# Differential attention in a two-layer trunk: score products that all use 128 rows, and heads that start one by one

## The chip, the cores and the metric

One core of a Trainium2 chip runs the whole kernel in one launch. The metric is the device time in microseconds of one execution. "Before" is the median of three runs.

## What is computed

Two layers, each a mixer of three parallel branches (a convolution module, a short gated convolution, differential attention with rotary positions) and an MLP, both with RMS norms and modulation by a conditioning vector. There are 512 tokens of width 1024, all in float32. The change touches the attention:

```python
N_HEADS = 8; HEAD_DIM = 64; V_HEAD_DIM = 128; Q_BLOCK = 128; DEPTH = 2

def diff_attention(q, k, v, lam, subln_g, lambda_init):
    # q, k: (1, 512, 8 heads, 2 parts, 64), turned by apply_rope before; v: (1, 512, 8, 128)
    for i in range(seq // Q_BLOCK):
        lo, hi = i * Q_BLOCK, (i + 1) * Q_BLOCK
        qb, kb, vb = q[:, lo:hi], k[:, :hi], v[:, :hi]
        s = jnp.einsum('bqhcd,bkhcd->bhcqk', qb, kb) * scale
        p = jax.nn.softmax(jnp.where(mask, s, -jnp.inf), axis=-1)
        a = p[:, :, 0] - lam * p[:, :, 1]
        outs.append(jnp.einsum('bhqk,bkhd->bqhd', a, vb))
    o = rmsnorm(jnp.concatenate(outs, axis=1), subln_g) * (1.0 - lambda_init)
```

Each head thus has two parts of 64 features, with a score matrix for each part, and block i of 128 queries sees the first 128 (i + 1) keys.

## The kernel before

**Products.** Activations lie with features on the partitions and the 512 tokens along the free axis. A float32 operand is split into a high part (rounded to float32r) and a low part (the rest), and a product is made of three passes: high x high, high x low, low x high. A projection of 128 output features takes 8 k-tiles x 3 passes = 24 matmuls of 512 columns into one of three PSUM banks, tag `mm`. Nearly all of them are issued in the helper `mm`, line 145, so they carry that line whatever they belong to. Weights come as raw tiles of 256 columns by DMA from SP's queue (line 367) and are split into `wh` (ScalarE, line 394) and `wl` (VectorE, line 402), with three tiles of each.

**Order.** The order of all five engines is the order of emission in Python. `mm` counts columns; each 4096 of them make a step (`STEP`), which is 8 matmuls of 512 columns. Everything that goes beside the projections is a generator in a heap of tasks: `yield n` means "not before n steps from now". So a task's place in every engine's queue follows from steps, and no engine reorders what was emitted.

**Queries and keys.** A layer's mixer goes through four pairs of heads. For each pair it makes four projections (queries and keys of the first head, then of the second) and the values. Each projection is followed by the task `rope`: ScalarE copies the PSUM bank out (line 712), four small DMAs swap halves (714), VectorE turns (717 to 720), ScalarE casts the high parts (723 and 724). To use all 128 rows of TensorE, for each part c the tile `d`c of the queries holds the high part twice, one copy above the other, and that of the keys holds the high part above the low part (or below it). One matmul of 128 rows is then high x high + high x low. The copies into the other half of the partitions are DMAs of 64 x 512 on SP (734 and 735). The low part of the queries lies once, both parts in one tile `lo` (728).

**Scores.** `attend` is the task of one head. For each of the four query blocks, and for each part c, it issues line 786 (128 rows, as above) and line 787: the queries' low part against the keys' high part, both 64 rows, on the half of the partitions where part c lies. Both sum into one bank of tag `s`, of which there are two, one for each part. After each block it stays away for `QSTEP` = 2 steps. `softmax` then reads the banks with VectorE (line 750, which frees them) and goes on with ScalarE (757) and VectorE (762 to 766). Then come the transposed weights (803), the products with the values (814, twelve of them, three for each key tile: 512, 384, 256 and 128 columns) and the norm of the head (822, 455).

**When a head begins.** The local task `pair` waits until all four tiles of the pair are there, then (first pair) `FIRST` = 2 more steps; it starts the first head, and `PERIOD` = 9 steps later the second. In layer 1 three projections (`NF`) are already made in the closing part of layer 0.

**Slots.** Tiles of tag `qk` take 16 slots in turn: a head uses five (two `d` and `lo` for queries, two `d` for keys), and a new tile waits until the one that had its slot 16 tiles ago has been read.

Of the kernel before, what the change touches and what calls it, by code (L numbers as in the profile page):

```python
# [10 lines left out]
F32 = mybir.dt.float32  # L11
# [12 lines left out]
NH = 8  # L24
# [6 lines left out]
# order of emission: columns of a step; steps between an event and what follows it  # L31
# [3 lines left out]
# the start: k-tiles of scale and shift of each quarter whose products VectorE makes, and the order  # L35
# [13 lines left out]
# the end of a sub-layer and the start of the next: the order  # L49
# [14 lines left out]
# columns of the per-layer parameter tile  # L64
C_BADA, C_NMIX, C_NMLP, C_CAB, C_LNG, C_LNB, C_CBW, C_SUB, C_FG = 0, 48, 56, 64, 68, 72, 76, 88, 89
NROW = 97
# order of the six adaLN vectors
# [4 lines left out]
def kernel(  # L72
# [46 lines left out]
    # ---------------------------------------------------------------- order of emission  # L119
    # Instructions are emitted in the order in which the engines run them. The products drive  # L120
    # a count of steps of STEP columns; what goes beside them waits in tasks, generators that
    # yield how many steps to stay away.
# [20 lines left out]
    def mm(ps, lhsT, rhs, start, stop, n):  # L143
        """a matrix product of the main stream"""
        T.matmul(ps, lhsT, rhs, start=start, stop=stop)  # L145
        clock[2] += n
        if clock[2] >= STEP:
            clock[2] -= STEP
            step()

    def pacer(p):
        """steps to wait, on average p() of them"""
        left = 0.0
        while True:
            left += p()
            n = int(left)
            left -= n
            yield n

    # ---------------------------------------------------------------- constants  # L160
# [17 lines left out]
    # ---------------------------------------------------------------- parameters  # L178
# [3 lines left out]
    def params(l, eng=None):  # L182
        """parameters by feature: rows in, transposed"""
# [42 lines left out]
    # lambda of the differential attention: -lambda on all partitions  # L226
# [29 lines left out]
    # ---------------------------------------------------------------- adaLN  # L256
# [5 lines left out]
    def ada_done(l, q, n, sm):  # L262
        """bias and what follows, of n of the columns of ada from column q"""
        v = q // 8
        dst = ada[l][:, q : q + n]
        ada_known[l].update(range(q, q + n))
        assert (l, 1 if v == SC_F else 0) in written and (l, 0) in written
        V.tensor_tensor(dst, sm, prm[l][:, C_BADA + q : C_BADA + q + n], op=ALU.add)
        if v in (SC_M, SC_F):
            f = (0 if v == SC_M else 8) + q % 8  # L270
            g0 = (C_NMIX if v == SC_M else C_NMLP) + q % 8
            V.scalar_tensor_tensor(out=gsc[l][:, f : f + n], in0=dst, scalar=1.0,
                                   in1=prm[l][:, g0 : g0 + n], op0=ALU.add, op1=ALU.mult)
        if v == G_M:
            V.tensor_scalar(out=dst, in0=dst, scalar1=0.5, scalar2=None, op0=ALU.mult)
# [8 lines left out]
    def ada_task(vs, pace):  # L284
        """task: vectors (layer, which) of adaLN, the products on VectorE, the sums over the
        partitions after a transpose"""
# [42 lines left out]
    # ---------------------------------------------------------------- weights  # L329
# [23 lines left out]
    # the raw tiles of 256 columns, and the halves of them in the order of their use  # L353
# [17 lines left out]
    def w_split(extra=None):  # L371
        """the next half of a raw tile as two parts; extra: a tag of
        slots that holds one beside the three of the pool"""
# [5 lines left out]
        if kk < 0:  # L379
            # the halves are rows  # L380
# [36 lines left out]
    def proj(ps, w, act, t0=0, t1=S, k0=0, k1=None):  # L417
        """a product, three passes of every k-tile"""
# [15 lines left out]
    # ---------------------------------------------------------------- helpers of the norms  # L434
    def rsqrt_small(v, n):
        """1/sqrt(v) for a small tile of positive numbers"""
        y = stile(n)
        G.tensor_tensor(y, v[:, :n], nhalf[:, :n], op=ALU.pow)  # L438
        return y

    def colsum(tiles, w, t0=0, t1=S):
        """means over the partitions of the tiles, tokens on partitions"""
# [8 lines left out]
    def bcast(col, n):  # L451
        """columns [tokens, n] to rows along all partitions, in PSUM"""
# [10 lines left out]
    def split(src, res, tags=("qk", "qk")):  # L463
        """task: src as two parts, put into the list res"""
# [7 lines left out]
    # ---------------------------------------------------------------- norm of x and modulation  # L472
    xT = [xpool.tile([P, S], F32, name=f"xT{k}") for k in range(KD)]

    def modulate(l, f, rb, hh, ks, t0=0, t1=S):
        """h tiles (hi, lo) of tokens t0:t1 from the broadcast 1/rms"""
# [25 lines left out]
    def sumsq(e, acc, t0, t1):  # L502
        """task: adds the squares of x tile e to acc"""
# [8 lines left out]
    def closing(lg, v, act, l, f, evac):  # L512
        """The product that closes a sub-layer, its residual gated by vector v of layer lg, and
        the norm of sub-layer f of layer l after it. The last two output tiles go in halves of the tokens, as do the first
        NF tiles of what follows, so that the norm of one half runs beside the products of the
        other. Returns h; evac takes the first tiles' products."""
# [84 lines left out]
    # ---------------------------------------------------------------- the end  # L601
    o2 = out.rearrange("b s d -> (b s) d")

    def ending_prepare(g):
        """task: x by token, and the rows of the last gains along all partitions"""
# [25 lines left out]
    def ending(act):  # L631
        """the last product, with the tokens on partitions, its residual, the last norm"""
# [70 lines left out]
    # ---------------------------------------------------------------- attention  # L703
# [3 lines left out]
    def rope(pp, res, j):  # L707
        """task: a tile of queries (j even) or keys (odd), turned. Queries: per part the high
        part twice one above the other, and the low part of both; keys: per part high and low
        part one above the other."""  # L710
# [15 lines left out]
        if j % 2 == 0:  # L726
            lo = slot("qk", F32R)
            V.tensor_tensor(lo, u, d0.bitcast(F32), op=ALU.subtract)
            src = (d0, d1)
        else:  # L730
            lo = u.bitcast(F32R)
            V.tensor_tensor(lo, u, d0.bitcast(F32), op=ALU.subtract)
            src = (u, u)
        nc.sync.dma_start(d0[64:, :].bitcast(F32), src[0][:64, :].bitcast(F32))
        nc.sync.dma_start(d1[:64, :].bitcast(F32), src[1][64:, :].bitcast(F32))
        yield RWAIT
        res.append((d0, d1, lo))
# [4 lines left out]
    def softmax(l, i, sps, l0, a):  # L742
        """task: query block i of a head"""
# [21 lines left out]
        # (softmax 0 - lambda softmax 1) times the sum of softmax 0  # L765
# [10 lines left out]
    def attend(l, hd, q, k, v, res):  # L776
        """task: one head"""
        a = []
        l0 = stile(4)
        for i in range(NTB):  # L780
# [3 lines left out]
            for cc in range(2):  # L784
                r = slice(64 * cc, 64 * cc + 64)
                T.matmul(sps[cc][:, :n], q[cc][:, blk], k[cc][:, :n], start=True, stop=False)  # L786
                T.matmul(sps[cc][:, :n], q[2][r, blk], k[cc][r, :n], start=False, stop=True)  # L787
# [3 lines left out]
        # transposed weights, keys on partitions  # L791
# [37 lines left out]
        # the mean square and eps, both times the squared sum of softmax 0  # L829
# [13 lines left out]
    # ---------------------------------------------------------------- mixer  # L843
    def mixer(l, h, qk, nfirst):
        """qk: the list for the first pair's queries and keys, nfirst of them under way"""
        oh = [None] * NH
        oo, glu, cv, yb, ya = [], [], [None] * 4, [], []
        # --- queries, keys, values
        for hp in range(NH // 2):
            if hp:  # L850
                qk, nfirst = [], 0
            for j in range(nfirst, 4):
                product(h, rope, qk, j)
            wv = [getw(), getw()]
            v2 = []
# [13 lines left out]
            def pair(hp, qk, v2):  # L869
                while len(qk) < 4:  # L870
                    yield 1
                if hp == 0 and FIRST:
                    yield FIRST
                spawn(attend(l, 2 * hp, qk[0], qk[1], v2, oh))
                yield PERIOD
                spawn(attend(l, 2 * hp + 1, qk[2], qk[3], v2, oh))

            spawn(pair(hp, qk, v2))
            run_due()

# [9 lines left out]
        # --- conformer convolution: gated linear unit  # L890
# [22 lines left out]
        def conv_norm():  # L913
            """layer norm of the convolution and its silu"""
# [66 lines left out]
        # --- short gated convolution  # L981
# [33 lines left out]
        # --- gates and merge  # L1015
# [34 lines left out]
    # ---------------------------------------------------------------- MLP  # L1050
# [9 lines left out]
    def mlp(l, h, f, nfirst):  # L1060
        """f: the list for the first hidden tiles, nfirst of them under way; returns the last"""
# [21 lines left out]
    # ---------------------------------------------------------------- the trunk  # L1083
# [6 lines left out]
    # --- the start: x by feature, and the first norm as fast as its adaLN vectors come in  # L1090
# [16 lines left out]
    def fetch(v, qt):  # L1107
        """a quarter of an adaLN vector: k-tiles 2j, 2j + 1 of 256 columns in tile j"""
# [23 lines left out]
    # rotary tables  # L1132
# [7 lines left out]
    def angles():  # L1140
        """task: the angles within half a turn; the cosine is the sine of a quarter turn more"""
# [26 lines left out]
    def partial(qt, vs):  # L1168
        """the products of the last k-tiles of a quarter, on VectorE; v: scale, shift"""
# [13 lines left out]
    def rows_of(qt, v, pt):  # L1183
        """sums over the partitions along all partitions, with the products of the other k-tiles"""
# [8 lines left out]
    def turn(row):  # L1193
        """by feature"""
# [26 lines left out]
    def warm(n):  # L1221
        """keeps TensorE's clock up while it has nothing to do"""
# [15 lines left out]
    # the first four chunks of weights: two parts, a quarter of their k-tiles at a time  # L1238
# [133 lines left out]
```

## Time and profile before

| | |
|---|---|
| Runs | 1935.61, 1937.01, 1938.61 us (median 1937.01) |
| Profiled execution: span from first to last instruction | 1935.4 us; the page gives no time of its own beside it |
| TensorE busy (PE) | 1914.2 us, 99% |
| VectorE (DVE), ScalarE (ACT), GpSimd (POOL) | 1246.5, 787.5, 60.6 us |
| Attention stage of layer 0 and of layer 1 | about 65 to 315 us and 1002 to 1262 us after the start |
| DMA moved | 236.99 MB, mean 122 GB/s |

PE is TensorE's matmuls, PEld its weight loads, which may run beside a matmul, SPq the DMA issues of SP. In rows by form, `64*128 64x512` is a weight tile of 64 rows and 128 columns with 512 columns that move through it, and the last columns are busy us, mean ns of one, and idle us ahead with what ended it. In the chain the columns are the start, the us that the piece adds to the path, and what it is. A wait for several semaphores is put down to the one that came last by the profile, which can be the wrong one when the engine named had long been done.

### The profile page before, as it was taken

The page shows a single profiled execution, that of the slowest core. Times are in us where ns is not written, and L with a number is a line of the kernel's source. Part 1 is how long each engine was busy: PE and PEld are TensorE (multiplying, and loading weights), DVE is VectorE, ACT ScalarE, POOL GpSimd, SP SyncE. Part 2 cuts the span into 40 slices and gives each one's busy share as a digit, 9 for nine tenths or more (in the row PEclk, how much of TensorE's full clock was granted, in tenths as well). Part 3 has the DMA queues.
Part 4 walks back from the last instruction along what each step waited for, and adds up shares of the span by engine and source line. Part 5 has one row for each costly group of instructions (what it writes and reads, how often), then busy time and mean ns, then how long its engine had stood idle before and what let it go on. Part 6 is the DMA issues. An engine that isn't in the chain of part 4 may idle for free.

```text
span 1935.4 us, 24880 instructions
## 1 busy us (share of the span) xinstructions
PE 1914.2 (99%) x9565; PEld 1602.8 (83%) x9565; DVE 1246.5 (64%) x2123; ACT 787.5 (41%) x1420; POOL 60.6 (3%) x109
## 2 busy tenths in 40 slices
PE   8999999999999999999999999999999999999998
PEld 6788878888889888888898788888888898888888
DVE  7776688997766656565676776898654563333335
ACT  4555553222433524243444655422243353324253
POOL 1001010000000000000000000000000000000000
PEclk9999999999999999999999999999999999999999
DMA  8633312353454456555534332123222422322321
GB/s 267 176 106 107 96 61 93 113 166 128 160 174 147 142 174 199 176 174 186 174 95 124 104 109 71 66 87 100 85 98 98 142 66 87 100 97 91 105 87 66
DMA packets 208965, 236.99 MB, mean 122 GB/s; under 512 B 9896, under 2 KB 177968, under 8 KB 208848
## 3 DMA queue, kind: packets, MB, share of 16 engines
q1 hardware_dynamic: 207920, 235.18, 38.5%
q8 instruction: 75, 1.23, 0.3%
q0 software_dynamic: 768, 0.23, 0.1%
q14 instruction: 42, 0.34, 0.1%
q10 hardware_dynamic: 160, 0.01, 0.0%
HBM read 216.50 MB, written 2.10 MB: 113 GB/s over the span
## 4 chain that ended last, share of the span: by engine, by line
PE 96%; DMA 2%; DVE 1%; POOL 0%; issue 0%; SPq 0%; ACT 0%; POOLq 0%; DVEq 0%; ACTq 0%
PE mm L145 85%; PE s L145 3%; PE s L787 2%; PE s L786 2%; PE t L814 2%; PE t L803 1%; DMA qk<-in_w_ada_dram 1%; PE t L455 1%; PE t L303 0%; PE t L822 0%; DMA o<-in_w_ada_dram 0%; POOL st L438 0%; DMA cv<-in_x_dram 0%; DMA raw<-in_w_in_dram 0%; SPq L714 0%
## 5 line engine op out<-in xcount | busy, mean ns | idle before, releaser
L145 PE MATMUL mm<-h,wh 128*128 128x512 f32 x2720 | 847.8, 392 | 0.0
L145 PEld LDWEIGHTS mm<-h,wh 128*128 128x128 f32 x2720 | 507.8, 188 | 104.2 <-issue 0.7
L145 PE MATMUL mm<-h,wl 128*128 128x512 f32 x1360 | 534.3, 393 | 0.0
L394 ACT CAST wh<-raw 128x1024 fp32r<-128x1024 f32 (+1 forms) x308 | 309.0, 1005 | 405.0 <-PE mm L145 358.9
L402 DVE TENSOR_TENSOR wl<-raw,wh 128x1024 fp32r<-128x1024 f32 (+1 forms) x308 | 357.8, 1165 | 70.5 <-ACT wh L394 67.2
L145 PEld LDWEIGHTS mm<-h,wl 128*128 128x128 f32 x1360 | 255.4, 188 | 54.7 <-issue 1.8
L145 PE MATMUL mm<-qk,wh 128*128 128x512 f32 (+1 forms) x1024 | 300.3, 376 | 0.0
L145 PEld LDWEIGHTS mm<-qk,wh 128*128 128x128 f32 x1024 | 188.2, 188 | 34.9
L145 PE MATMUL mm<-qk,wl 128*128 128x512 f32 (+1 forms) x512 | 192.6, 376 | 0.0
L906 DVE SCALAR_TENSOR_TENSOR cv<-v,caw,cv 128x511 f32<-128x511 f32 (+14 forms) x240 | 175.8, 733 | 4.2
L499 DVE SCALAR_TENSOR_TENSOR xT<-mm,ada,xT 128x512 f32<-128x512 f32 (+1 forms) x81 | 55.9, 691 | 148.6 <-PE mm L145 148.5
L281 DVE SCALAR_TENSOR_TENSOR araw<-araw,cact,araw 128x512 f32<-128x512 f32 x140 | 104.4, 746 | 26.0 <-DMA araw<-in_w_ada_dram 25.6
L145 PEld LDWEIGHTS mm<-qk,wl 128*128 128x128 f32 x512 | 96.3, 188 | 17.4
L1053 ACT ACTIVATE f<-mm 128x512 f32<-128x512 f32 x60 | 35.9, 598 | 160.6 <-PE mm L145 160.6
L145 PE MATMUL mm<-o,wh 128*128 128x512 f32 (+1 forms) x320 | 95.5, 381 | 0.0
L145 PE MATMUL mm<-v,wh 128*128 128x512 f32 (+1 forms) x320 | 94.9, 379 | 0.0
L757 ACT ACTIVATE cv<-cv,st 128x128 f32<-128x128 f32 (+3 forms) x128 | 71.2, 558 | 39.2 <-DVE st L750 38.7
L145 PE MATMUL mm<-wh,h 128*128 128x256 f32 x448 | 85.0, 285 | 0.0
L1027 DVE SCALAR_TENSOR_TENSOR f<-f,mm 128x512 f32<-128x512 f32 x38 | 26.1, 687 | 83.6 <-PE mm L145 83.5
L750 DVE CUSTOM_DVE_ANT_0 cv<-s,mask 128x128 f32<-128x128 f32 (+3 forms) x128 | 59.0, 486 | 30.1 <-PE s L787 29.4
L469 DVE TENSOR_TENSOR qk<-f,qk 128x512 fp32r<-128x512 f32 x38 | 26.3, 691 | 77.3 <-ACT qk L466 77.3
L438 POOL TENSOR_TENSOR st<-st,nhalf 128x4 f32<-128x4 f32 (+2 forms) x29 | 30.8, 1063 | 1364.5 <-DVE st L460 1009.8
(258 smaller groups left out, 2297.0 us busy)
## 6 DMA issues: line engine op xcount, KB each, us to landing
raw<-in_w_in_dram SPq DMA_DIRECT2D x66, 1024.0 KB, 5.2
raw<-in_w_ff_dram SPq DMA_DIRECT2D x64, 1024.0 KB, 5.3
araw<-in_w_ada_dram SPq DMA_DIRECT2D x160, 256.0 KB, 3.0
f<-f SPq DMA_DIRECT2D x128, 64.0 KB, 2.0
raw<-in_w_c_out_dram SPq DMA_DIRECT2D x8, 1024.0 KB, 4.9
raw<-in_w_out_dram SPq DMA_DIRECT2D x8, 1024.0 KB, 4.9
qk<-in_w_ada_dram SPq DMA_DIRECT2D x16, 256.0 KB, 6.0
qk<-qk SPq DMA_DIRECT2D x32, 128.0 KB, 2.4
```

The lines of the kernel that those rows point to most:

```text
L145: T.matmul(ps, lhsT, rhs, start=start, stop=stop)
L281: V.scalar_tensor_tensor(out=part, in0=r, scalar=cact[:, k : k + 1], in1=part, op0=ALU.mult, op1=ALU.add)
L394: A.copy(h_, r_)
L402: V.tensor_tensor(l_, r_, h_.bitcast(F32), op=ALU.subtract)
L499: V.scalar_tensor_tensor(out=xT[e][:, t0:t1], in0=pp[:, t0:t1], scalar=g[:, e : e + 1], in1=xT[e][:, t0:t1], op0=ALU.mult, op1=ALU.add)
L750: V.tensor_tensor_reduce(out=pp[:, :n], in0=sps[cc][:, :n], in1=mask[:, S - n :], op0=ALU.add, op1=ALU.min, scale=-0.125, scalar=3.0e38, a ...
L757: A.activation(p[cc][:, :n], p[cc][:, :n], AF.Exp, bias=nb[:, cc : cc + 1], scale=-1.0, accum_out=l0[:, i : i + 1] if cc == 0 else s1)
L786: T.matmul(sps[cc][:, :n], q[cc][:, blk], k[cc][:, :n], start=True, stop=False)
L787: T.matmul(sps[cc][:, :n], q[2][r, blk], k[cc][r, :n], start=False, stop=True)
L814: T.matmul(po[:, j * P :], v[j // 2][x_][:, c0 : c0 + P], tiles[j][y_], start=j == 0 and i == 0, stop=j == NTB - 1 and i == 2)
L906: V.scalar_tensor_tensor(out=ac[:, s:], in0=glu[j][:, : S - s], scalar=wk, in1=ac[:, s:], op0=ALU.mult, op1=ALU.add)
L1053: A.activation(r, pp, AF.Relu)
```

## The change

The low part of the queries gets the same layout as the high part: for each part c a tile `e`c that holds it twice, one copy above the other, and the second score product takes `e`c against the keys' whole tile `d`c. It now has 128 rows and adds low x low, which the kernel before left out. For it `rope` takes one more subtraction on VectorE and two more DMAs per query tile, and one more slot: six a head. The task `pair` is gone; one task `heads` goes through the eight heads and starts each one when its own queries and keys are there, at least `PERIOD` steps after the one before. The comments are gone from the file too, and lines behind line 725 are numbered a few higher.

```diff
@@ rope
         if j % 2 == 0:
-            lo = slot("qk", F32R)
-            V.tensor_tensor(lo, u, d0.bitcast(F32), op=ALU.subtract)
-            src = (d0, d1)
+            e0, e1 = slot("qk", F32R), slot("qk", F32R)
+            V.tensor_tensor(e0, u, d0.bitcast(F32), op=ALU.subtract)
+            V.tensor_tensor(e1[64:, :], u[64:, :], d1[64:, :].bitcast(F32), op=ALU.subtract)
+            moves = ((d0, d0, d1, d1), (e0, e0, e1, e1))
+            parts = (d0, d1, e0, e1)
         else:
             lo = u.bitcast(F32R)
             V.tensor_tensor(lo, u, d0.bitcast(F32), op=ALU.subtract)
-            src = (u, u)
-        nc.sync.dma_start(d0[64:, :].bitcast(F32), src[0][:64, :].bitcast(F32))
-        nc.sync.dma_start(d1[:64, :].bitcast(F32), src[1][64:, :].bitcast(F32))
+            moves = ((d0, u, d1, u),)
+            parts = (d0, d1)
+        for a0, b0, a1, b1 in moves:
+            nc.sync.dma_start(a0[64:, :].bitcast(F32), b0[:64, :].bitcast(F32))
+            nc.sync.dma_start(a1[:64, :].bitcast(F32), b1[64:, :].bitcast(F32))
         yield RWAIT
-        res.append((d0, d1, lo))
+        res.append(parts)
@@ attend
             for cc in range(2):
-                r = slice(64 * cc, 64 * cc + 64)
                 T.matmul(sps[cc][:, :n], q[cc][:, blk], k[cc][:, :n], start=True, stop=False)
-                T.matmul(sps[cc][:, :n], q[2][r, blk], k[cc][r, :n], start=False, stop=True)
+                T.matmul(sps[cc][:, :n], q[2 + cc][:, blk], k[cc][:, :n], start=False, stop=True)
@@ mixer
+        pairs = []
+        def heads():
+            for hd in range(NH):
+                while len(pairs) <= hd // 2 or len(pairs[hd // 2][0]) < hd % 2 * 2 + 2:
+                    yield 1
+                if hd == 0 and FIRST:
+                    yield FIRST
+                qk, v2 = pairs[hd // 2]
+                spawn(attend(l, hd, qk[hd % 2 * 2], qk[hd % 2 * 2 + 1], v2, oh))
+                yield PERIOD
+        spawn(heads())
         for hp in range(NH // 2):
             if hp:
                 qk, nfirst = [], 0
+            v2 = []
+            pairs.append((qk, v2))
...
-            def pair(hp, qk, v2):
-                while len(qk) < 4:
-                    yield 1
-                if hp == 0 and FIRST:
-                    yield FIRST
-                spawn(attend(l, 2 * hp, qk[0], qk[1], v2, oh))
-                yield PERIOD
-                spawn(attend(l, 2 * hp + 1, qk[2], qk[3], v2, oh))
-            spawn(pair(hp, qk, v2))
-            run_due()
```

Three places of the program show what moves. In these rows a tile is named by its tag and a running number, the result stands before the arrow, and the size is that of the result. First TensorE at the first score block of layer 0; `mm_860` before and `mm_866` after are the same projection, the first one behind the values of pair 0, and `qk_758` and `qk_759` are the keys of head 0. Before:

```order
L145 MATMUL mm_860<-h_238,wh_674 128x512
L145 MATMUL mm_860<-h_239,wh_674 128x512
L145 MATMUL mm_860<-h_238,wl_697 128x512
L786 MATMUL s_888<-qk_758,qk_729 128x128
L787 MATMUL s_888<-qk_758,qk_762 128x128
L786 MATMUL s_889<-qk_759,qk_730 128x128
L787 MATMUL s_889<-qk_759,qk_762 128x128
L145 MATMUL mm_901<-h_224,wh_699 128x512
```

After:

```order
L145 MATMUL mm_866<-h_228,wh_674 128x512
L145 MATMUL mm_866<-h_229,wh_674 128x512
L789 MATMUL s_878<-qk_758,qk_729 128x128
L790 MATMUL s_878<-qk_758,qk_762 128x128
L789 MATMUL s_879<-qk_759,qk_730 128x128
L790 MATMUL s_879<-qk_759,qk_763 128x128
L145 MATMUL mm_866<-h_228,wl_697 128x512
L145 MATMUL mm_866<-h_230,wh_674 128x512
```

The block stood behind all 24 matmuls of the projection and now stands behind the first 8, so 16 matmuls of 512 columns (two steps) come after it rather than before. In layer 1 the first block moves ahead by four steps in the same way. The second head moves like the first; the later ones stay where they were in layer 0 and move by two steps in layer 1.

Second, SP's queue at the queries and keys of heads 0 and 1 in layer 0 (`f_676` and `f_738` hold the keys). Before:

```order
L735 DMA qk_759<-f_676 64x512
L734 DMA qk_786<-qk_786 64x512
L735 DMA qk_787<-qk_787 64x512
L734 DMA qk_813<-f_738 64x512
L735 DMA qk_814<-f_738 64x512
```

After:

```order
L739 DMA qk_763<-qk_763 64x512
L738 DMA qk_758<-f_676 64x512
L739 DMA qk_759<-f_676 64x512
L738 DMA qk_790<-qk_790 64x512
L739 DMA qk_791<-qk_791 64x512
L738 DMA qk_821<-qk_821 64x512
L739 DMA qk_822<-qk_822 64x512
L738 DMA qk_817<-f_738 64x512
L739 DMA qk_818<-f_738 64x512
```

Ahead of each head's two key transfers there now stand four transfers of its queries, not two.

Third, VectorE at the same tiles, where `f_704` is the swapped copy of the last of the four projections and `f_676` the key tile of head 0. Before:

```order
L728 TENSOR_TENSOR qk_762<-f_640,qk_729 128x512
L719 TENSOR_TENSOR f_704<-f_704,sin_t 128x512
L720 TENSOR_TENSOR f_738<-f_738,f_704 128x512
L732 TENSOR_TENSOR f_676<-f_676,qk_758 128x512
L253 COPY nlam<-t_782 128x2
```

After:

```order
L728 TENSOR_TENSOR qk_762<-f_640,qk_729 128x512
L729 TENSOR_TENSOR qk_763<-f_640,qk_730 64x512
L719 TENSOR_TENSOR f_704<-f_704,sin_t 128x512
L720 TENSOR_TENSOR f_738<-f_738,f_704 128x512
L734 TENSOR_TENSOR f_676<-f_676,qk_758 128x512
L253 COPY nlam<-t_786 128x2
```

The subtraction for `e1` is new and stands between `e0` and the turning of the last key tile; the rest keeps its order.

More of the change, by code (lines that the diff above doesn't have):

```diff
@@ L854, in mixer @@
             wv = [getw(), getw()]
-            v2 = []
             for bb in range(2):
```

## Prediction

> **What bounds the kernel now.** I read the page first: the busy shares, the chain that ended last, the granted clock.
>
> ```profile
> PE 1914.2 (99%) x9565; PEld 1602.8 (83%) x9565; DVE 1246.5 (64%) x2123; ACT 787.5 (41%) x1420; POOL 60.6 (3%) x109
> PEclk9999999999999999999999999999999999999999
> PE 96%; DMA 2%; DVE 1%; POOL 0%; issue 0%; SPq 0%; ACT 0%; POOLq 0%; DVEq 0%; ACTq 0%
> PE mm L145 85%; PE s L145 3%; PE s L787 2%; PE s L786 2%; PE t L814 2%; PE t L803 1%; DMA qk<-in_w_ada_dram 1%; PE t L455 1%; PE t L303 0%; PE t L822 0%; DMA o<-in_w_ada_dram 0%; POOL st L438 0%; DMA cv<-in_x_dram 0%; DMA raw<-in_w_in_dram 0%; SPq L714 0%
> ```
>
> TensorE is on the path for 96% of the span at full clock, so a change pays if it shortens TensorE's own stream, and costs if it makes TensorE wait. The score products (L786 and L787) are about 4% of the chain. Busy time does not tell what they cost, since the ends of matmuls are modelled; I take the chain in order of time, whose first column is the start and whose second is what the piece adds to the path. These are the rows of the last head of layer 1: the first row of each score block, the row behind the block, and four plain rows for comparison.
>
> ```profile
> 1199.12 0.06 PE s L786
> ...
> 1199.95 3.85 PE mm L145 x16
> ...
> 1204.24 0.12 PE s L786
> ...
> 1205.29 0.59 PE t L822 x4
> ...
> 1210.02 0.18 PE s L786
> ...
> 1211.31 0.37 PE t L803 x2
> 1211.67 3.66 PE mm L145 x16
> 1215.34 0.23 PE s L786
> ...
> 1216.84 5.71 PE mm L145 x24
> 1222.55 1.85 PE t L814 x12
> ...
> 1228.99 0.44 PE t L822 x4
> ...
> 1233.55 0.22 PE t L803 x2
> ```
>
> A plain 512-column product costs 3.66/16 = 0.229 us. A block of four score products takes 0.83 us (128 keys), 1.05 (256), 1.29 (384) and 1.50 (512), the differences of the starts. The row behind each block is also long: 3.85 against 3.66 for 16 products, 0.59 against 0.44 for four transposes, 0.37 against 0.22 for two, 5.71 against 24 x 0.229 = 5.49; that adds 0.19, 0.15, 0.15 and 0.22. One head's 16 score products therefore cost 4.67 + 0.71 = 5.38 us.
>
> The L814 row is the yardstick: 12 products with 128 rows, three each of 512, 384, 256 and 128 columns, in 1.85 us. Sixteen products of the same four sizes at that price are 1.85 x 4/3 = 2.47 us. So a head pays 2.91 us over it. The weight loads show where, here in a 512-column block (the bracket is TensorE's load side idle before the load):
>
> ```profile
> 1111.92 0.18 PEld L787 LDWEIGHTS s<-qk,qk 64*128 64x128 f32 x1 [0.25 <-issue]
> 1112.34 0.19 PEld L786 LDWEIGHTS s<-qk,qk 128*128 128x128 f32 x1 [0.24 <-DVE f L732]
> 1112.77 0.18 PEld L787 LDWEIGHTS s<-qk,qk 64*128 64x128 f32 x1 [0.25 <-issue]
> 1113.20 0.19 PEld L145 LDWEIGHTS mm<-wl,h 128*128 128x128 f32 x1 [0.24 <-issue]
> 1113.31 0.31 PEld L145 LDWEIGHTS mm<-wh,h 128*128 128x128 f32 x2
> ```
>
> At each step from 128 rows to 64 or back, four times a block, the load waits until the array is free and its 0.18 to 0.19 us lie open; between two products of 128 rows (last row) the next load follows without a gap. Four times 0.18 is 0.72, near the 0.6 to 0.8 that a block is too long.
>
> **The change part by part.**
>
> *All score products with 128 rows.* L787's 64-row products get a doubled low part as their weights, so no step between row counts is left. The sum: 16 heads x 2.91 = 46.6 us off the path. Nothing else fills these gaps, as TensorE runs in order. If 128-column products were bound by the transposes' 0.11 (0.44/4) and 256 by 0.12, a block set would be 0.229 + 0.172 + 0.12 + 0.11 = 0.63, a head 2.52, and the gain 45.8. I take 46.6, since L814 holds just these sizes.
>
> *One more subtraction a head on VectorE* (L729, 64x512). The nearest rows are the 128x512 subtraction and ScalarE's cast of 64 rows, which is no shorter than one of 128:
>
> ```profile
> L728 DVE TENSOR_TENSOR qk<-f,qk 128x512 fp32r<-128x512 f32 x16 | 10.9, 684 | 0.0
> L724 ACT CAST qk<-f 64x512 fp32r<-64x512 f32 x32 | 19.7, 617 | 0.6
> 64.70:315.00 250.30, 248.80 (x1290) 201.08 (x1291) 182.00 (x404) 136.28 (x326) 21.86 (x43) 1.00 0.34 97
> 252.00:278.00 26.00, 26.00 (x121) 20.07 (x121) 22.46 (x51) 15.51 (x39) 2.49 (x4) 1.00 0.26 82
> ```
>
> I take 0.68 us, 5.5 us a layer. The third row is the attention stage of layer 0 (length, then busy time of PE, PEld, DVE, ACT, POOL, clock, DMA share): VectorE has 182.0 of 250.3. Afterwards it has 187.5 in about 250 - 23 + 4 = 231, 81%. Cost zero on average, covered by VectorE's idle fifth. The cover is thinnest at the last head (fourth row): 22.46 of 26.0 becomes some 22.5 to 23.1 of 23.1.
>
> VectorE also frees the two score banks between blocks. The tightest place I found is the third block of head 0:
>
> ```profile
> 90.69 0.55 DVE L750 CUSTOM_DVE_ANT_0 cv<-s,mask 128x384 f32<-128x384 f32 x1
> 92.38 0.39 PE L786 MATMUL s<-qk,qk 128*128 128x512 f32 x1
> ```
>
> The bank is free at 91.24 and used at 92.38: 1.14 us spare. A 384-column block shrinks by 1.44 - 4 x 0.172 = 0.75, so it holds. Cost zero, at most 1 us there in each layer if the added subtraction falls before it.
>
> *Two more transfers a head* (64x512, 128 KB), 32 in all, on SP, which takes 0.5 to 0.6 us to issue each (rows below). The DMA engines are busy a third of the stage (0.34 above), so their time is hidden; what is moved is the key's transfers, which now stand behind four of the query's rather than two. Weight and swap transfers later in SP's order move by the same 1.2 us a head; they lead by a product or more, so zero.
>
> *Six slots a head instead of five, of 16.* A key tile now takes the slot of the head two before. In layer 0 ScalarE's casts of the keys of heads 3, 5 and 7 now wait for the last score block of heads 1, 3 and 5, which stands just ahead of them in emission; ScalarE has 136 of 250 us to do and the keys are wanted nine steps (some 20 us) later. Zero.
>
> *A head begins when its own queries and keys are there.* In the order of instructions head 0's first block moves ahead by 16 products (two steps) in layer 0 and by four steps in layer 1; the later heads keep their place or move by two steps. Only head 0 is near its data:
>
> ```profile
> 64.68 11.43 PE mm L145 x72
> 72.72 0.69 DVE L719 TENSOR_TENSOR f<-f,sin_t 128x512 f32<-128x512 f32 x1 [1.69 <-DMA f<-f]
> 74.05 0.68 DVE L732 TENSOR_TENSOR f<-f,qk 128x512 fp32r<-128x512 f32 x1
> 74.76 0.46 SPq L734 DMA_DIRECT2D qk<-f  x1
> 75.28 0.59 SPq L735 DMA_DIRECT2D qk<-f  x1
> 77.60 0.30 PE L786 MATMUL s<-qk,qk 128*128 128x128 f32 x1 [1.50 <-ACT f L712]
> ```
>
> TensorE ends its products at 76.11 and waits 1.5 us. ScalarE, which the row names, was long done; what lands last is the key's transfer, issued at 74.76 and there 2.84 later. That time does not move: it hangs on L732, behind L719, which waits for another tile's swap (72.72), and the added subtraction fits into the 1.69 idle ahead of that; the low part's two transfers are issued about 72.2 to 73.4, done by then. But TensorE now arrives 16 x 0.229 = 3.66 us earlier, at 72.45. The wait grows from 1.5 to 5.15, and the 16 products that covered it come afterwards: **+3.66 us**, on the path. The bounds are 0 (data earlier by as much, for which no row speaks) and 4.9 (both added issues ahead of the key's). In layer 1:
>
> ```profile
> 1010.62 0.50 SPq L734 DMA_DIRECT2D qk<-qk  x1
> 1014.45 0.54 SPq L734 DMA_DIRECT2D qk<-f  x1
> 1020.18 0.63 PE L145 MATMUL mm<-h,wh 128*128 128x512 f32 x2
> 1025.65 0.22 PE L786 MATMUL s<-qk,qk 128*128 128x128 f32 x1
> ```
>
> The block would stand four steps, 16,384 columns, ahead of 1025.65: the 24 products since 1020.18 and 16 of 256 columns before (16 x 0.12 = 1.9), so at 1018.3. The key's transfer goes out 1.2 later than 1014.45 and lands 2.84 after, at 1018.5; its second part 0.6 later, while the first two products take 0.2. **+0.65 us**, between 0 and 1.8.
>
> The sum: 1935.4 - 46.6 + 3.66 + 0.65 = 1893.1 us of span. The page gives no time beside the span; the runs' median, 1937.01, lies 1.6 above it and the lowest run 0.2. With 1.6 I forecast 1894.7, rounded 1895.
>
> **The rivals.**
>
> *No gain, and the longer waits remain: slower.* The load could lie open behind every score product whatever its rows, because the weights change between a high and a low tile of the queries; then all 128 rows save nothing, and 3.66 + 0.65 = 4.3 us are added: 1941.3. It decides when under 9% (4.3 of 46.6) of the open loads go. Against it stand the last load row above and L814, which alternates high and low tiles without a gap. The Trainium skill, "TensorE: Matmul & The Clock Gate", Part 3, "The mechanism", says that a weight load overlaps running products only when its row group differs. By that rule products that all use the same rows would never hide a load, and this rival's 1941.3 would come out; the trace disagrees, with loads of 128 rows hidden at 0.229 us a product. Chance 0.04.
>
> *Half the gain.* Of the four open loads of a block two belong to L786 or follow a wait for the bank (the label DVE on the second load row); if these stay open because of the wait, half remains: 1894.7 + 23.3 = 1918. Against it: the L145 load behind the block waits for no bank and idles the same 0.24. Chance 0.06.
>
> *VectorE sets the end in the shorter stage.* For it speaks the 252 to 278 window, against it the 81% of the stage. If each head loses what VectorE gains in work, 16 x 0.68 = 11 us: 1906. Chance 0.10.
>
> **How the numbers follow.** My forecast, all loads hidden and both first waits, has 0.79; its own range is 1890 (no longer waits) to 1900 (bounds of the waits, and a microsecond or two at the banks). The remaining 0.01 is no change. About 0.2%, 4 us, is what a measurement of this kernel can tell. Range 1890 to 1907, which takes in VectorE's case and leaves out 0.11. Faster: 0.79 + 0.10 + 0.06 = 0.95; same 0.01; slower 0.04.
>
> **What would show it.** The chain should have score blocks of about 0.4, 0.5, 0.7 and 0.9 us with no long row behind them, and the load side no idle time there. The first score product of layer 0 should still start near 77.6, with an idle of about 5 us before it; in layer 1 under 2 us. VectorE should have 16 operations more, SP 32 issues more. The forecast is wrong if loads stay open at 128 rows, if TensorE waits for a bank or a weight tile in the attention stage, or if head 0's data come earlier or later than before.

## The result and the profile after

| | before | after |
|---|---|---|
| Median (runs) | 1936.72 us (4; 1935.61 to 1938.61) | 1904.72 us (4; 1902.72 to 1913.19) |
| Ratio, 95% interval | | 0.9845 (0.9824 to 0.9866) |
| Profiled execution: its time, its span | span 1935.4 us | 1904.28 us, span 1902.5 us |

The kernel is 32 us faster, about 10 us less than forecast. The span fell by 32.9 us where 42.3 were worked out. One run among the experiments below, of the kernel with `FIRST` = 3, was slow (2329.19 us at a granted clock of 0.75) and is left out of that kernel's median.

First the page after: the busy line and the chain's shares by engine.

```profile
PE 1874.3 (99%) x9565; PEld 1599.9 (84%) x9565; DVE 1256.0 (66%) x2139; ACT 785.8 (41%) x1420; POOL 63.4 (3%) x109
PE 93%; DMA 3%; DVE 2%; issue 1%; SPq 1%; ACT 1%; POOL 0%; POOLq 0%; DVEq 0%; ACTq 0%
```

VectorE has its 16 operations more. TensorE's share of the path fell from 96% to 93%, and DMA, VectorE and SP's queue took over: somewhere TensorE now waits for a chain of those. The gain itself is where it was forecast. These are the rows of the chain for the last head of layer 1, each score block's first row, the row behind it, and one plain row.

```profile
1165.55 0.06 PE s L789
...
1165.95 3.74 PE mm L145 x16
...
1170.13 0.12 PE s L789
...
1170.61 0.44 PE t L825 x4
...
1175.17 0.18 PE s L789
...
1175.88 0.22 PE t L806 x2
1176.10 3.65 PE mm L145 x16
1179.74 0.23 PE s L789
...
1180.65 5.44 PE mm L145 x24
```

The blocks take 0.40, 0.48, 0.71 and 0.91 us by the differences of the starts, 2.50 together, and only the first has a slightly long row behind it (3.74 against 3.65); the others are plain. Forecast was 2.47 a head. The weight loads show the same. These are all loads of the second score product, before and after (count, then busy us and mean ns of one, then the load side's idle us ahead of them):

```profile
L787 PEld LDWEIGHTS s<-qk,qk 64*128 64x128 f32 x128 | 23.4, 183 | 23.2 <-issue 17.5
L790 PEld LDWEIGHTS s<-qk,qk 128*128 128x128 f32 x128 | 24.4, 191 | 1.7
```

With 128 rows, 1.7 of the 23.2 us of idle time are left.

What was not forecast stands in the list of waits (total us, times, longest). First two of TensorE's rows and one of VectorE's, after; then the same VectorE row of before, whose TensorE waits hold no row for a score bank.

```profile
PE s L789 <- DVE st L754: 5.6, 5, 2.2
PE s L789 <- DMA qk<-f: 3.4, 2, 3.2
DVE f L719 <- DMA f<-f: 13.5, 10, 2.6
```

```profile
DVE f L719 <- DMA f<-f: 9.9, 7, 3.1
```

TensorE waits five times, 5.6 us in all, for a score bank that VectorE has to free (L754). VectorE itself waits 13.5 us at the product with the sine (L719) for the swapped copy, which the four small DMAs of `rope` (L714) bring; they are called the swap below. It did so for 9.9 us before too, and then TensorE had no wait for a bank. The largest of the five, in layer 1, shows how the two hang together: VectorE's rows, TensorE's row at that place, and the swap's row in the chain there.

```profile
1023.64 0.75 DVE L770 SCALAR_TENSOR_TENSOR cv<-cv,st,cv 128x512 f32<-128x512 f32 x1
1026.34 0.69 DVE L719 TENSOR_TENSOR f<-f,sin_t 128x512 f32<-128x512 f32 x1 [1.95 <-DMA f<-f]
1027.07 0.69 DVE L720 TENSOR_TENSOR f<-f,f 128x512 f32<-128x512 f32 x1
1027.67 0.28 DVE L754 CUSTOM_DVE_ANT_0 cv<-s,mask 128x128 f32<-128x128 f32 x1
1028.02 0.39 PE L789 MATMUL s<-qk,qk 128*128 128x256 f32 x1 [2.16 <-DVE st L754]
1020.23 5.99 DMA f<-f
1028.76 3.29 PE mm L145 x8
```

The maxima of the 128-key block (L754) free the banks. They stand in VectorE's queue behind L719 and L720, and L719 stands idle 1.95 us for a swap transfer that took 5.99 us. The median of these transfers is a third of that, and two weight tiles of 1 MB went out just ahead, as SP's row and the page's list of issues (KB each, median us to landing) show; the DMA engines were busy for a share of 0.99 of the time from 1020 to 1025 us. That the weights slow the swap is read from this; no run moves them.

```profile
1014.77 1.51 SPq L367 DMA_DIRECT2D raw<-in_w_in_dram  x2
f<-f SPq DMA_DIRECT2D x128, 64.0 KB, 2.0
```

The chain runs through a slow swap at the other four waits too: at 113.49, 1075.89 and 1123.55 us in the same way (swaps of 4.63, 6.15 and 6.68 us; waits of 0.68, 0.57 and 1.10), and at 102.90 us (5.96; 1.07) by way of ScalarE's casts, which follow L720 and hold up the weight split (L402) ahead of the maxima. None of the five waits is in head 0: two fall on head 1 of layer 0, the others on heads 1, 3 and 5 of layer 1.

The last row shown above is a second loss: 8 products behind the wait take 3.29 us, not 8 x 0.229 = 1.83. The same stands behind the first wait of layer 0, here TensorE's row, the chain's row for the 16 products behind it, and the windows around both places (length, busy time of PE, PEld, DVE, ACT, POOL, then the granted clock, the DMA share and GB/s):

```profile
76.10 0.30 PE L789 MATMUL s<-qk,qk 128*128 128x128 f32 x1 [3.19 <-DMA qk<-f]
77.31 4.97 PE mm L145 x16
75.00:80.00 5.00, 3.77 (x11) 3.11 (x12) 2.12 (x7) 0.99 (x4) 0.00 (x0) 0.66 0.79 200
1027.50:1032.00 4.50, 3.98 (x13) 3.13 (x14) 3.05 (x8) 3.53 (x8) 0.43 (x2) 0.64 0.43 95
```

The granted clock was 0.66 and 0.64 there, where the attention stages of the kernel before have 1.00 in every 5 us; it cost 4.97 - 3.66 = 1.3 us and 3.29 - 1.83 = 1.5 us.

### The profile page after: what moved, and what is told of

It reads as the page before. It is cut to its first block, busy times and chain, and to the rows that moved or that the text cites. A ratio compares the mean times of both kernels' runs of the same rounds, so it can differ in the third digit from the quotient of the medians.

```text
span 1902.5 us, 24972 instructions
## 1 busy us (share of the span) xinstructions
PE 1874.3 (99%) x9565; PEld 1599.9 (84%) x9565; DVE 1256.0 (66%) x2139; ACT 785.8 (41%) x1420; POOL 63.4 (3%) x109
## 4 chain that ended last, share of the span: by engine, by line
PE 93%; DMA 3%; DVE 2%; issue 1%; SPq 1%; ACT 1%; POOL 0%; POOLq 0%; DVEq 0%; ACTq 0%
PE mm L145 83%; PE s L145 3%; DMA f<-f 2%; PE t L817 1%; PE s L789 1%; PE s L790 1%; PE t L806 1%; SPq L714 1%; PE t L1193 1%; PE t L455 0%; PE t L303 0%; PE t L825 0%; POOL st L438 0%; DVE f L719 0%; PE t L1214 0%
## 5 line engine op out<-in xcount | busy, mean ns | idle before, releaser
L402 DVE TENSOR_TENSOR wl<-raw,wh 128x1024 fp32r<-128x1024 f32 (+1 forms) x308 | 358.2, 1166 | 69.6 <-ACT wh L394 65.9
L469 DVE TENSOR_TENSOR qk<-f,qk 128x512 fp32r<-128x512 f32 x38 | 26.3, 691 | 77.4 <-ACT qk L466 77.2
L145 PEld LDWEIGHTS mm<-wh,h 128*128 128x128 f32 x448 | 70.8, 191 | 0.4
```

Source lines behind the costliest of these rows:

```text
L402: V.tensor_tensor(l_, r_, h_.bitcast(F32), op=ALU.subtract)
L469: V.tensor_tensor(lo, src, hi.bitcast(F32), op=ALU.subtract)
```

## The experiments

**First round: is it the new start, or the added work?** My first theory put the bank waits down to the earlier place of heads 0 and 1; its rival to the added subtraction, transfers and slots. Four kernels take the change apart. The first has 128 rows with both heads of a pair started together, as before:

```diff
-FIRST = 2
+FIRST = 1
-        spawn(heads())
...
+            spawn(pair(hp, qk, v2))
+            run_due()
```

> The scores with 128 rows as in the changed kernel, but the start of the heads as before: both heads of a pair begin when all four of its tiles are there, with FIRST = 1 in place of 2, so that head 0's blocks stand one step (8 products, 1.83 us) earlier than in the kernel before in layer 0 and in layer 1, where the changed kernel has them two and four steps earlier. Theory (the rows bring the gain of about 46 us, and the early place of heads 0 and 1 costs what is missing: first wait, waits for a score bank behind swap transfers, granted clock lost after them): first wait in layer 0 about 1.5 + 1.8 = 3.3 us, no wait in layer 1, bank waits under 1.5 us in all; 1936.7 - 46.6 + 1.8 = about 1892, 1889 to 1896. Rival (the bank waits come from the added subtraction and transfers, wherever the heads stand): bank waits of 4 to 6 us remain, 1897 to 1903.

Measured: 1901.62 us (1901.4 to 1904.32), ratio 0.9822 (0.9808 to 0.9835). This misses my theory, and the rival's range holds it. With head 0 only one step early in both layers the bank waits stay; the same list of waits (the second row is the first wait of layer 0):

```profile
PE s L789 <- DVE st L754: 5.9, 8, 1.6
PE s L789 <- issue: 1.4, 1, 1.4
```

The next two keep the changed kernel's start. One has the old scores altogether, the other pays for all the added work and undoes only the row count:

```diff
 e2: old rope (one low tile, two transfers) and
 e3: new rope, but both with
-                T.matmul(sps[cc][:, :n], q[2 + cc][:, blk], k[cc][:, :n], start=False, stop=True)
+                T.matmul(sps[cc][:, :n], q[2 + cc][r, blk], k[cc][r, :n], start=False, stop=True)
```

> The new start of the heads alone: score products with 64 rows, one low tile, two transfers and five slots a head as before. Theory (the early place costs what is missing): no gain, the first waits, some bank waits and the lost clock are added: 1936.7 + 4 to 9 = 1941 to 1946. Rival (the bank waits come from the added subtraction and transfers): the first waits alone, 1936.7 + 3 to 4 = 1940 to 1941, with hardly any wait for a score bank.

> The changed kernel with one thing undone: the second score product takes the 64 rows of its own part of the doubled low tiles; subtraction, transfers, slots and start stay. Its distance to the changed kernel (1904.7) is the price of the row change alone: theory 46.6, 1951 if all waits stay, less if the longer blocks cover waits for a bank, so 1946 to 1951. Its distance to the kernel with the new start alone is the price of the added subtraction, transfers and slots: theory 0 to 2 us; rival (these make the bank waits) 4 to 8 us. If the row change itself brings clearly less than forecast, this kernel stands at 1940 to 1945.

Measured: 1942.56 us (ratio 1.0031, 1.0019 to 1.0042) and 1942.93 us (1.0029, 1.0016 to 1.0041), against 1936.39 for before on this chip. So the new start alone costs 6 us, and the added subtraction, transfers and slots show no cost (0.4 us, within the intervals): the rival falls as well. The second time also lies below the 1946 to 1951 us of the theory: it is 38 us above the changed kernel, not 46.6, as the changed kernel pays for waits that this one does not have. The waits of the two, first without and then with the added work:

```profile
PE s L789 <- DMA qk<-f: 3.1, 1, 3.1
```

```profile
PE s L790 <- DMA qk<-f: 4.7, 1, 4.7
PE s L790 <- DVE st L754: 0.5, 1, 0.5
```

With 64-row blocks there is no bank wait in the one and 0.5 us in the other, though the heads start at the changed kernel's places. The fourth kernel moves the heads by a step:

```diff
-FIRST = 2
+FIRST = 3
```

> The changed kernel with FIRST = 3 in place of 2: heads 0 to 7 begin one step (8 products, 1.83 us) later in both layers, so that head 0 stands one step earlier than in the kernel before in layer 0 and three in layer 1. Theory (the early place costs): layer 0's first wait falls from 3.2 us to about 1.5 and its clock is kept, bank waits become fewer; 1904.7 - 2 to 6 = 1899 to 1903. Rival (the place is not the cause): 1904 to 1906, the waits merely stand elsewhere.

Measured: 1899.16 us, ratio 0.9806 (0.9791 to 0.9821), better than the changed kernel by 5.6 us. The time is the theory's, its terms are not: the bank waits fell from 5.6 to 3.1 us, but the first wait was 2.6 us, not 1.5, and the 8 products behind it still took 3.43 us. The place seems to have a share, but does not account for the waits.

**Second round: shorter blocks, and a VectorE that stands at a wait.** A third theory: the bank waits come from the gain itself. Blocks that are 0.7 us shorter, one after the other, bring TensorE to the banks earlier, and VectorE, held by the swap transfers, does not come earlier. Two kernels leave work out to test this. The first leaves out the added work, and with it the low part of the queries in the scores; the second leaves out the swap from the second pair on, so it multiplies unswapped tiles (`hp`, the number of the pair, is handed to `rope`):

```diff
 e5
 ...
-            moves = ((d0, d0, d1, d1), (e0, e0, e1, e1))
-            parts = (d0, d1, e0, e1)
+            moves = ((d0, d0, d1, d1),)
+            parts = (d0, d1, d0, d1)
 ...
 e6
-        for q in range(4):
+        for q in range(0 if hp else 4):
 ...
-        V.tensor_tensor(sw, sw, sin_t, op=ALU.mult)
+        V.tensor_tensor(sw, t if hp else sw, sin_t, op=ALU.mult)
```

> The changed kernel with 128-row products and the new start, but without the added work: no fourth query tile, no added subtraction, no added transfers, five slots a head as before; the second score product takes the high part once more as its weights, so the low part of the queries is left out of the scores. Theory (the shorter score blocks bring TensorE to the two score banks earlier, and VectorE, held up by swap transfers, frees them no earlier): the bank waits of 5.6 us remain, 4 to 6, and the time is 1902 to 1905. Rival (added subtraction, transfers and slots make them): bank waits under 1 us, clock kept in layer 1, 1904.7 - 5.6 - 1.5 = about 1897, 1896 to 1899.

> The changed kernel without the swap transfers of the later pairs: from the second pair of each layer on, the product with the sine takes the unswapped tile and the four transfers for it are left out, so VectorE never waits for them; the first pair is as it was. Theory (VectorE stands idle at the product with the sine, waiting for the swap behind the weight transfers, and the score maxima that free the banks stand behind it): bank waits under 1 us, first wait in layer 0 as before, 1904.7 - 5 - 1.5 = about 1898, 1896 to 1900. Rival (VectorE has too much to do in these stretches and would be late without the wait): bank waits of 3 us or more remain, 1901 to 1905.

Measured: 1903.95 us without the added work (ratio 0.9825, 0.981 to 0.984), not told apart from the changed kernel, with bank waits of 7.7 us; 1896.23 us without the later pairs' swaps (0.9789, 0.9772 to 0.9805), with no bank wait left. TensorE's row of the first, VectorE's row of the second:

```profile
PE s L788 <- DVE st L753: 7.7, 5, 2.5
```

```profile
DVE f L719 <- DMA f<-f: 3.6, 3, 2.1
```

So 128 rows make the waits without any added work, and they go when VectorE no longer stands at the swap. The second also takes transfers off the queue, so it does not part VectorE's wait from the traffic. But if the wait is the cause, nothing need be left out: it should do to let VectorE come to L719 later.

```diff
         V.tensor_tensor(u, t, cos_t, op=ALU.mult)
-        yield 2
+        yield 3 if hp else 2
         V.tensor_tensor(sw, sw, sin_t, op=ALU.mult)
```

> The changed kernel with the product with the sine one step (1.83 us) later in the later pairs of each layer (three steps after the product with the cosine, not two), so that VectorE does other work while the swap is under way; nothing is left out. Theory (VectorE waits there with the maxima behind it): half or more of the bank waits go, 1904.7 - 3 to 7 = 1898 to 1902. Rival (what is later by a step is missed elsewhere, the keys of the next head or the slots): no better, 1904 to 1907.

Measured: **1895.49 us** (1894.6 to 1897.17), ratio 0.9785 (0.9771 to 0.98), span 1893.7 us: 9 us under the changed kernel, and better than the 1898 to 1902 expected. TensorE has no bank wait left. VectorE's rows and TensorE's at the place shown above:

```profile
1022.34 0.29 DVE L754 CUSTOM_DVE_ANT_0 cv<-s,mask 128x128 f32<-128x128 f32 x1
1022.82 0.69 DVE L719 TENSOR_TENSOR f<-f,sin_t 128x512 f32<-128x512 f32 x1
1022.98 0.36 PE L789 MATMUL s<-qk,qk 128*128 128x256 f32 x1
```

The maxima now stand ahead of L719, which finds its copy there, and the 256-key block follows without a wait.

**Third round: what the rows are worth, and what is left.** The same kernel with half rows prices the row change with no bank wait on either side, and the kernel before with the later step alone is the control.

> The kernel with the product with the sine a step later (1895.5 us), with one thing undone: the second score product takes only the 64 rows of its own part. Without waits for a bank on either side the distance is the price of the row change alone. Theory (the forecast's 46.6 us holds once nothing eats it): 1895.5 + 45 to 48 = 1940 to 1944. Rival (the rows are worth only what the changed kernel showed against its own version with half rows, 1942.9 - 1904.7 = 38 us, and the later step brings 9 us by itself): about 1934.

> The kernel before with only the product with the sine a step later in the later pairs. Theory (with the long score blocks TensorE never waits for a bank, so VectorE's waits for the swap cost nothing): 1936 to 1938, no change against 1936.7. Rival (the later step is worth some 9 us in any kernel): about 1928.

Measured: 1941.74 us (1.0021, 1.0012 to 1.003) and 1937.88 us (1.0004, 0.9996 to 1.0013). Against before on its own chip (1937.46 and 1936.77) the one is 4.3 us slower and the kernel with full rows 41.3 faster: the rows are worth 45.6 us (the ends of the two intervals allow 41 to 50). The later step by itself is worth nothing, though VectorE's waits at L719 fell from 9.9 to 4.1 us with it (and two waits for a bank, 0.8 us together, came up); it only gives back what the shorter blocks had lost.

What remained was the first wait of layer 0 and the clock behind it. One kernel fills the wait with transposes; it ran once in the changed kernel and then, in more runs, with the later step. Another starts the heads a step later.

```diff
 e8, and with the later step e12
+            if l == 0 and hd == 0 and i == 0:
+                pt = ps_t()
+                for _ in range(26):
+                    T.transpose(pt[:, :P], ident, ident)
             sps = [ps_s(), ps_s()]
 e11: the later step and
-FIRST = 2
+FIRST = 3
```

> The changed kernel with 26 transposes of a constant tile (0.11 us each, 2.9 us) ahead of head 0's first score block in layer 0, where TensorE waits 3.2 us for the key. Theory (the granted clock falls because TensorE stands idle): wait of 0.3 to 1 us, clock 0.95 or more in the 5 us behind it against 0.66, the 16 products behind the block in 3.7 us against 4.97, end about 1.3 us earlier. Rival (the clock falls for another reason): still 0.6 to 0.8 there, 16 products in about 5 us.

> The kernel with the product with the sine a step later, with 26 transposes of a constant tile (2.9 us) ahead of head 0's first score block in layer 0, where TensorE waits 3.3 us and the 16 products behind the block then took 5.30 us against 3.66. Theory (the idle time lowers the granted clock): wait under 1 us, clock 0.95 or more in the 5 us behind it, the 16 products in 3.7 to 4.0 us, 1895.5 - 1.5 = about 1894. Rival (the clock falls there for another reason): 16 products still in about 5 us, 1895 to 1896.

> The changed kernel with both: the product with the sine a step later, and FIRST = 3, so that head 0's blocks stand 8 products later. Theory (what is left against the sum of gains is the first wait of layer 0, 3.3 us, and the clock lost behind it, 1.6): wait about 1.5 us, the 16 products behind the block in under 4.2 us, 1895.5 - 1.8 - 1.0 = about 1892.5, 1891 to 1894. Rival (a later start of the heads brings waits of its own, as the changed kernel with FIRST = 3 showed 1.1 us for the weights' transposes): 1895 to 1898.

The single run gave 1906.17 us. Its key came at 77.4 us rather than 76.1, so 2.5 us of wait were left behind the transposes and the 16 products still took 5.22 us; it decides nothing. With the later step: 1896.41 us (0.979, 0.9777 to 0.9803), no better than without transposes, but the clock tells. The window and the 16 products behind the block, first without transposes (wait 3.3 us), then with them (wait 0.8):

```profile
75.00:80.00 5.00, 4.05 (x13) 3.26 (x14) 1.88 (x7) 0.88 (x4) 0.00 (x0) 0.70 0.76 186
76.80 5.30 PE mm L145 x16
```

```profile
75.00:80.00 5.00, 4.11 (x26) 3.41 (x24) 2.23 (x7) 0.90 (x4) 0.00 (x0) 1.00 0.94 216
77.94 3.71 PE mm L145 x16
```

The clock stayed at 1.00 and the products took 3.71 us rather than 5.30. At this place it is the idle time that lowers the clock, as far as one profiled execution can show it. About 1.1 of the 1.6 us were lost again because the key landed that much later in this execution: one issue on SP ahead of it took 1.87 us rather than 0.52. In the single run a swap of 3.64 us was late instead; whether the transposes have to do with either stays open. The start with FIRST = 3 gave 1895.16 us (0.9782, 0.9768 to 0.9795), which is the rival's number: the wait fell to 1.6 us, but 8 products behind it still took 3.36 us, and bank waits of 2.0 us came back. Between these three versions the runs show no difference.

## Why the prediction was right, and by how much it was off

The measured 1904.72 us lies 10 us above the forecast and inside the range of 1890 to 1907, but outside the 1890 to 1900 that the forecast claimed for itself. The range holds it only because it was widened for the rival "VectorE sets the end", and that is luck, as will be seen. Two of the three signs that the prediction named for being wrong came as well: TensorE waits for a bank, and head 0's data come earlier than before. By the prediction's own steps, with the profiled execution's numbers:

| term | forecast | measured |
|---|---|---|
| score rows | -46.6 | -45.6 (from two kernels without bank waits) |
| first wait, layer 0 | +3.66 | 3.2 - 1.5 = +1.7 |
| granted clock behind it | not a term | +1.3 |
| first wait, layer 1 | +0.65 | +0.2 |
| waits for a score bank | 0, at most 1 in each layer | +5.6 |
| granted clock behind the longest of them | not a term | +1.5 |
| added subtraction, transfers, slots | 0 | +0.4, no difference |

These add up to -34.9 against the span's -32.9, so about 2 us stay unassigned.

The mechanism of the gain and its price held: 2.50 us a head, and 1.7 us of idle load side ahead of all the second products. The Trainium skill's rule on weight loads ("TensorE: Matmul & The Clock Gate", Part 3, "The mechanism"), by which products that use the same rows would never hide one, does not hold here: 16 loads of 0.19 us alone would take 3.0 us, more than the 2.50 of a head's products.

The step that failed is the one that costed VectorE's freeing of the banks at zero. It looked at one block, the third of head 0, and set that block's shrink of 0.75 us against 1.14 us of slack. That block held; the waits, 5.6 us and the clock behind the longest, came in later heads. There TensorE is early by all the shorter blocks ahead, not by one, as the theory has it; no run parts the blocks. And it took VectorE's row at L750 as fixed at an engine's pace, with the stage's busy share (81%) as the argument. At all five waits the chain leads back to a swap: VectorE was not short of time; it stood idle for a transfer. The list of VectorE's own waits, 9.9 us at L719 before, was the warning that a sooner TensorE might have to pay for such waits. "VectorE sets the end" was a rival at 1906, near the measured time, but by the wrong mechanism: it charged each head the added subtraction, which costs nothing that the runs show. VectorE set the end at five blocks only, through the swap.

The first wait of layer 0 was mis-sized (+3.66 for a measured +1.7), as its premise was wrong that the key's time does not move. VectorE's row ahead of it, after the change, has no wait left:

```profile
71.19 0.69 DVE L719 TENSOR_TENSOR f<-f,sin_t 128x512 f32<-128x512 f32 x1
```

It had waited 1.69 us for its swap and started at 72.72; now the copy was there, and the score block began 1.5 us earlier (76.10). Why the copy came sooner stays open. It is no sure gain: in the single run with transposes VectorE waited 1.58 us at this place again and began at 72.54. The clock was missing from the sum. The Trainium skill, "TensorE: Matmul & The Clock Gate", Part 1, "What's actually happening", says that TensorE falls to half rate after an idle window of about 3.4 us, and that the windows run freely. The traces agree on the fall, with a granted clock of 0.66 in the 5 us around the end of the 3.2 us wait, and of 0.50 from 77.5 to 80.0 us in the kernel with the later step; but waits of 2.16 and of 1.6 us were enough too.

The layer-1 wait, the slots and the transfers came out as argued or smaller.

## What to carry to other kernels

When the bounding engine gets shorter work, add up how much earlier it comes to each later meeting point, and hold that against the other engines' own waits, not against their busy shares: an engine that stands at a slow transfer has slack that nobody uses until someone comes early. If an instruction that waits stands in a queue ahead of one that others need, put it later: here one step gave back 9 us. A wait of a few microseconds on TensorE can cost more than its length, so it belongs into the sum with the clock that may fall behind it.

## What the hardware showed that I had not expected

Waits of 1.4 to 3.3 us on TensorE were followed by some 5 us at a clock of 0.64 to 0.75, at a price of 1.3 to 1.7 us each (the shortest, 1.41 us in layer 1 of the kernel with the old start, with a clock of 0.66). It does not follow from the length alone: in the kernel before, 1.5 us of idle time cost nothing (the 16 products behind took 3.83 us), and in the kernel without the added work a wait of 1.96 us lowered the clock and a longer one, of 2.48 us, did not. These are TensorE's rows at the two waits; of the windows, two are the first place and what followed, two the second:

```profile
114.61 0.57 PE L788 MATMUL s<-qk,qk 128*128 128x512 f32 x1 [1.96 <-DVE st L753]
1030.55 0.39 PE L788 MATMUL s<-qk,qk 128*128 128x256 f32 x1 [2.48 <-DVE st L753]
110.00:115.00 5.00, 3.04 (x25) 2.74 (x23) 2.91 (x8) 2.04 (x4) 0.00 (x0) 0.99 0.12 35
115.00:120.00 5.00, 5.00 (x28) 4.71 (x27) 4.77 (x17) 2.61 (x8) 0.00 (x0) 0.67 0.24 52
1025.00:1030.00 5.00, 3.07 (x16) 2.35 (x14) 2.64 (x6) 0.59 (x1) 0.00 (x0) 1.00 0.55 116
1030.00:1035.00 5.00, 4.45 (x24) 3.79 (x24) 3.55 (x11) 3.54 (x8) 0.43 (x2) 1.00 0.35 77
```

What decides it stays open. And 64 KB transfers that land in 2.0 us by the median took 4.63 to 6.68 us at the five waits; in the 4 us before the swap's issue, SP had sent out two weight tiles of 1 MB each time, and one ahead of the 4.63.
